# Last two heads of a grouped-query attention written as one sequence with three PSUM banks, in a two-layer hybrid attention kernel

## Chip, core and metric

The kernel runs on one core of a Trainium2 chip, as one launch. The metric is device time in microseconds: 1148.67 us is the median of 3 runs of the kernel before (1148.1 to 1149.11). TensorE (PE) multiplies matrices; its weight loads stand in a row of their own (PEld) and overlap the products. VectorE (DVE), ScalarE (ACT) and GpSimd (POOL) do the elementwise work, SyncE (SP) issues nearly all transfers. Each engine works through its own list of instructions in order. Products are summed in PSUM, which has eight banks of 128 x 512 fp32; the other tiles lie in SBUF.

## What is computed

Two layers act on 512 latent and 256 context tokens of width 1024. Each layer has a neighbourhood attention (branch a) and a grouped-query attention (branch b, 8 query heads on 2 key/value heads, 64 wide); both read all context keys. Each branch's output is multiplied by its own SiLU gate, projected, and the two are merged:

```python
def _merge(a_att, b_att, a_z, b_z, g_a, g_b, w_o_a, w_o_b, w_out):
    o_a = (a_att * jax.nn.silu(a_z)) @ w_o_a
    o_b = (b_att * jax.nn.silu(b_z)) @ w_o_b
    merged = jax.nn.sigmoid(g_a) * o_a + jax.nn.sigmoid(g_b) * o_b
    return merged @ w_out
```

The first layer also updates the context (its context queries read context keys alone), the second, which is the last, doesn't. So layer 0 works on 768 tokens, layer 1 on 512 wherever only queries are concerned.

## The kernel before

**Precision.** Each fp32 operand is split into a high part (a cast on ACT) and a low part (the rest, a subtraction on DVE or POOL), and a matrix product is three PE products: high x high, low x high, high x low (`mm3`, L351 to L353).

**The grouped-query attention** (called gq below, from L934 on) runs head by head in `pipeline` (L837). For head h, `gq_scores` makes four tiles of scores of 128 queries x 768 keys (L718, L719), DVE takes the row maximum (L955), ACT the exponential (L957), and DVE (L656) or POOL (L658, L659) scales the rows: POOL those of tiles 1 and 3 (`GQ_POOL`). One step later `gq_values` (L963) treats head h-1 in six **blocks** k of 128 keys: four PE transposes of the scaled tiles into one bank (L669), ACT's cast of that bank to `pth` (L672), DVE's subtraction to `ptl` (L673), and two products into the head's sum (L972, L973). In layer 0 a seventh block does the context queries (L746, L747). The transposes have two banks (`pst`), `pth` and `ptl` two buffers each. `head_out` (L675) ends a head: ACT copies half of the sum (L681), DVE adds the other half (L682), POOL multiplies into `zb` (L683), the gate of branch b.

**Filling products.** `fill` is a list of the remaining gate projections and of branch a's output projection (`o_chunks("a", ...)`, sums in `psf`, inputs `gah` and `gal`, evacuated on DVE in L592). `pipeline` runs an eighth of it per head, and all that is left ahead of head 7's values. A compiling scheduler then sets the order on each engine from the dependences and the order of the code, so filling products stand well ahead of where the code has them; `in_program_order` and `behind` can pin an order.

**After head 7**, `early` has loaded the gates of the merge (`tg`) and split the first three quarters of `zb` into `gbh` and `gbl` (`hilo`: ACT casts in L557, POOL subtracts in L558); the fourth quarter, heads 6 and 7, follows in L1002. Branch b's output projection (`o_chunks("b", ...)`: `gbh` and `gbl` by `w_o_b`, eight groups of 128 channels, four k steps of three products each) is evacuated by `evac_b` (L1005): DVE in L1007 and L1008, ACT in L1010, DVE in L1011. Its sums lie in a pool of five banks (`psx`) opened once the attention's banks are given back (`open_ps`), and in the one bank `psf`. Weights come by SP's queue; ACT casts (L336, L321) and DVE or POOL subtracts (L338, L324); `whi` and `wlo` have eight buffers each. Last comes the output projection of 128 tokens at a time (`tok_proj`, two halves of 512 columns), with `evac_o` (L1037): a DVE multiply (L1039), a DVE addition (L1041) and, in layer 1, the store (L1043).

## Time and profile before

| | |
|---|---|
| median of 3 runs | 1148.67 us (1148.1 to 1149.11) |
| the profiled execution | 1149.07 us |
| its span in the trace | 1147.0 us, so 2.07 us lie around it |
| granted TensorE clock | 0.999 |
| busy time | PE 1123.5, PEld 949.2, DVE 818.3, ACT 580.3, POOL 483.0 us |

A row of the timeline gives the start in us from the span's start, the duration, the engine and line, what is written from what, shapes and count; in brackets stands the idle time ahead of it and what ended it. PE's durations overlap: how long one product really takes is the distance to the next start. A row of the windows gives busy time and number of instructions of each engine in one stretch. A row of the waits gives the sum, the number of times and the longest.

### The profile page before, as it was taken

The page shows a single profiled execution, that of the slowest core. Times are in us where ns is not written, and L with a number is a line of the kernel's source. Part 1 is how long each engine was busy: PE and PEld are TensorE (multiplying, and loading weights), DVE is VectorE, ACT ScalarE, POOL GpSimd, SP SyncE. Part 2 cuts the span into 40 slices and gives each one's busy share as a digit, 9 for nine tenths or more (in the row PEclk, how much of TensorE's full clock was granted, in tenths as well). Part 3 has the DMA queues.
Part 4 walks back from the last instruction along what each step waited for, and adds up shares of the span by engine and source line. Part 5 has one row for each costly group of instructions (what it writes and reads, how often), then busy time and mean ns, then how long its engine had stood idle before and what let it go on. Part 6 is the DMA issues. An engine that isn't in the chain of part 4 may idle for free.

```text
span 1147.0 us, 17434 instructions
## 1 busy us (share of the span) xinstructions
PE 1123.5 (98%) x6136; PEld 949.2 (83%) x6136; DVE 818.3 (71%) x1533; ACT 580.3 (51%) x1185; POOL 483.0 (42%) x449
## 2 busy tenths in 40 slices
PE   7999999999999999999999999999999999999998
PEld 5788888888988888888788787888888888887786
DVE  6777688997454786697588755469787665898563
ACT  6553366655433565665330355336666355766421
POOL 1073355453374343453411227345554664465311
PEclk9999999999999999999999999999999999999999
DMA  9645311333322232451434424633332333152143
GB/s 370 232 127 156 90 51 60 105 110 111 106 101 89 95 103 92 92 221 38 149 127 130 151 70 122 193 89 115 97 113 74 111 102 101 65 176 90 61 133 92
DMA packets 89695, 135.08 MB, mean 118 GB/s; under 512 B 10789, under 2 KB 52745, under 8 KB 88969
## 3 DMA queue, kind: packets, MB, share of 16 engines
q1 hardware_dynamic: 89328, 133.87, 36.8%
q8 instruction: 48, 0.79, 0.3%
q14 instruction: 39, 0.31, 0.1%
q10 hardware_dynamic: 280, 0.12, 0.0%
HBM read 116.63 MB, written 17.32 MB: 117 GB/s over the span
## 4 chain that ended last, share of the span: by engine, by line
PE 80%; DVE 7%; DMA 4%; issue 3%; ACT 3%; POOL 2%; SPq 0%; POOLq 0%; ACTq 0%; DVEq 0%
PE psx L353 12%; PE psx L352 12%; PE psx L351 11%; PE psf L351 9%; PE psf L352 9%; PE psf L353 9%; PE pst L669 4%; DMA raw<-in_w_in_dram 2%; PE pss L718 2%; PE pss L719 2%; PE psv L973 2%; PE psv L972 1%; PE pss L795 1%; PE pst L431 1%; DMA rawb<-in_w_ada_dram 1%
## 5 line engine op out<-in xcount | busy, mean ns | idle before, releaser
L673 DVE TENSOR_TENSOR ptl<-pst,pth 128x512 fp32r<-128x512 f32 (+1 forms) x176 | 115.9, 671 | 46.4 <-ACT pth L672 45.4
L672 ACT CAST pth<-pst 128x512 fp32r<-128x512 f32 (+1 forms) x176 | 99.3, 577 | 86.7 <-PE pst L669 55.8
L338 POOL TENSOR_TENSOR wlo<-raw,whi 128x512 fp32r<-128x512 f32 x68 | 95.6, 1409 | 105.1 <-ACT whi L336 83.9
L351 PE MATMUL psf<-hx,whi 128*128 128x512 f32 (+1 forms) x368 | 139.2, 378 | 0.6 <-ACT zt L516 0.6
L352 PE MATMUL psf<-hx,whi 128*128 128x512 f32 (+1 forms) x368 | 138.2, 375 | 0.0
L353 PE MATMUL psf<-hx,wlo 128*128 128x512 f32 (+1 forms) x368 | 137.8, 374 | 0.0
L351 PE MATMUL psx<-whi,hx 128*128 128x512 f32 (+1 forms) x368 | 137.6, 375 | 0.0
L353 PE MATMUL psx<-whi,hx 128*128 128x512 f32 (+1 forms) x368 | 135.9, 369 | 0.1
L352 PE MATMUL psx<-wlo,hx 128*128 128x512 f32 (+1 forms) x368 | 135.7, 369 | 0.0
L336 ACT CAST whi<-raw 128x512 fp32r<-128x512 f32 x136 | 82.7, 621 | 51.6 <-DMA raw<-in_w_in_dram 35.6
L321 ACT CAST whi<-raw 128x512 fp32r<-128x512 f32 x88 | 53.9, 623 | 99.6 <-PE psx L353 38.1
L669 PE MATMUL pst<-ident,p 128*128 128x128 f32 x640 | 99.9, 272 | 1.4 <-DVE ptl L673 0.8
L324 POOL TENSOR_TENSOR wlo<-raw,whi 128x512 fp32r<-128x512 f32 x36 | 50.9, 1416 | 110.0 <-ACT whi L321 74.6
L338 DVE TENSOR_TENSOR wlo<-raw,whi 128x512 fp32r<-128x512 f32 x68 | 68.6, 1010 | 28.1 <-ACT whi L336 27.2
L669 PEld LDWEIGHTS pst<-ident,p 128*128 128x128 f32 x640 | 77.8, 140 | 13.0 <-DVE ptl L673 1.3
L658 POOL TENSOR_SCALAR r<-r 128x1 f32<-128x1 f32 x64 | 22.4, 350 | 152.2 <-DVE r L653 145.2
L659 POOL TENSOR_TENSOR p<-p,r 128x512 f32<-128x512 f32 (+1 forms) x64 | 84.2, 1316 | 5.1
L353 PEld LDWEIGHTS psx<-whi,hx 128*128 128x128 f32 x368 | 69.4, 189 | 12.6 <-DVE hx L1137 1.0
L351 PEld LDWEIGHTS psx<-whi,hx 128*128 128x128 f32 x368 | 69.5, 189 | 12.4 <-issue 0.8
L353 PEld LDWEIGHTS psf<-hx,wlo 128*128 128x128 f32 x368 | 69.4, 188 | 11.8
L351 PEld LDWEIGHTS psf<-hx,whi 128*128 128x128 f32 x368 | 69.4, 189 | 11.4 <-ACT zt L516 0.8
L352 PEld LDWEIGHTS psx<-wlo,hx 128*128 128x128 f32 x368 | 69.5, 189 | 10.8
(252 smaller groups left out, 3056.0 us busy)
## 6 DMA issues: line engine op xcount, KB each, us to landing
raw<-in_w_in_dram SPq DMA_DIRECT2D x168, 256.0 KB, 2.9
rawb<-in_w_ada_dram SPq DMA_DIRECT2D x64, 256.0 KB, 2.9
gs<-zt SPq DMA_DIRECT2D x32, 256.0 KB, 2.1
raw<-in_w_out_dram SPq DMA_DIRECT2D x32, 256.0 KB, 2.9
tg<-gs SPq DMA_DIRECT2D x4, 1536.0 KB, 6.8
rawx<-in_w_ada_dram SPq DMA_DIRECT2D x8, 512.0 KB, 7.9
raw<-in_w_o_a_dram SPq DMA_DIRECT2D x16, 256.0 KB, 2.8
raw<-in_w_o_b_dram SPq DMA_DIRECT2D x16, 256.0 KB, 2.8
```

The lines of the kernel that those rows point to most:

```text
L321: S.copy(hi[:, :n], raw[:, :n])
L324: e.tensor_tensor(lo[:, :n], raw[:, :n], F(hi[:, :n]), ALU.subtract)
L336: S.copy(hi, raw)
L338: lo_eng(i).tensor_tensor(lo, raw, F(hi), ALU.subtract)
L351: T.matmul(ps, lhs[0], rhs[0], start=first, stop=False)
L352: T.matmul(ps, lhs[0], rhs[1], start=False, stop=False)
L353: T.matmul(ps, lhs[1], rhs[0], start=False, stop=last)
L659: G.tensor_tensor(p[:, c0:c1], p[:, c0:c1], r[:, i:i + 1].to_broadcast([128, c1 - c0]), ALU.mult)
L669: T.transpose(pt[:, c0:c0 + 128], src, ident)
L672: S.copy(hi[:, n0:n1], pt[:, n0:n1])
L673: V.tensor_tensor(lo[:, n0:n1], pt[:, n0:n1], F(hi[:, n0:n1]), ALU.subtract)
L718: T.matmul(ps[:, c0:c0 + n], q, sl(kh), start=True, stop=False)
```

## The change

**Heads 6 and 7.** `pipeline` gets a `tail`. After head 7's scores it calls `gq_tail`, which has both heads' values as one list of blocks: six of head 6, in layer 0 the two heads' context blocks, six of head 7. Three banks and three pairs of buffers go round: the two `pst` banks and one of the score banks; the third pair comes from the weights' `whi` and `wlo`. Three blocks are transposed and split in advance, and block b+3 is transposed behind the products of block b. What is left of `fill`, and behind it the steps of `early`, stand among the first five blocks. The products of the first three o_b groups, k steps 0 to 2, follow the last block; then the fourth quarter of `gbh` and `gbl` and their last k step. PE, ACT and DVE keep the written order in this stretch. For these two heads DVE does the multiplies into `zb` (was POOL) and the last subtraction of `gbl`; the weights of the first two o_b chunks are loaded ahead of the tail with POOL's subtraction; POOL scales head 7's tiles 0 and 2 instead of 1 and 3.

**Last token tile** of layer 1's last half: two sums of 256 columns with an evacuation and a store each.

```diff
+                    if h == 7 and tail is not None:
+                        run(bg, len(bg))
+                        return tail(prev, st, fill, last)
...
-                    softmax_tail(p, 768, r[:, 0:1], [(0, 768)], G if i in GQ_POOL else None)
+                    softmax_tail(p, 768, r[:, 0:1], [(0, 768)], G if i in ((0, 2) if att["h"] == 7 else GQ_POOL) else None)
...
+            lead = [(f, 0, 512) for f in range(3)]
...
+            def gq_tail(st6, st7, fill, after):
+                need_wb(0, pool_lo)
...
+                banks = [psw(512, "t"), psw(512, "t"), psw(512, "s")]
+                s1 = psw(512, "s")
+                extra = fill + after
...
+                parts = [[att["p"].tile([128, 512], F32R, tag=t, name=nm(t), bufs=att["nt"]) for t in ("pth", "ptl")]
+                         for i in range(2)]
+                parts.append([wp.tile([128, 512], F32R, tag=t, name=nm(t), bufs=8) for t in ("whi", "wlo")])
+                po6 = psw(512, "v")
...
+                def gate_part(c0, c1):
+                    hi, lo = [a[:, 3, c0:c1] for a in gated["b"]]
+                    S.copy(R(hi), zv[:, 3, c0:c1])
+                    V.tensor_tensor(R(lo), zv[:, 3, c0:c1], hi, ALU.subtract)
...
+                def turn_block(b):
+                    if b < len(blocks):
+                        pt, (hi, lo) = banks[b % 3], parts[b % 3]
+                        for src, c0 in blocks[b][0]:
+                            T.transpose(pt[:, c0:c0 + 128], src, ident)
+                        S.copy(hi, pt)
+                        V.tensor_tensor(lo, pt, F(hi), ALU.subtract)
+                for b in range(3):
+                    turn_block(b)
+                for b, (_, mm, out) in enumerate(blocks):
+                    mm(*parts[b % 3])
+                    turn_block(b + 3)
+                    if out:
+                        out()
+                    run(extra, -(-len(extra) // max(5 - b, 1)) if b < 5 else 0)
+                    if first and b == 9:
+                        gate_part(512, 768)
+                for (f, n0, n1), ps in zip(lead, (po6, s1, psw(512, "s"))):
+                    chan_mm(ps, wb[f // 2], f % 2, act_b, n0, n1, 0, 3)
+                    open_sums.append((f, n0, n1, ps))
+                gate_part(0, 512)
+                in_program_order((ON_PE, ON_ACT, ON_DVE), nc.cur_bb.bb.instructions[at:], {ON_PE: before.name})
+                for f, n0, n1, ps in open_sums:
+                    chan_mm(ps, wb[f // 2], f % 2, act_b, n0, n1, 3, 4)
...
+            for f, n0, n1, ps in open_sums:
+                evac_b(f, n0, n1, ps)
...
+                    if not first and n == 1 and t == nt - 1:
+                        for c in ((0, 256), (256, 512)):
+                            ps = psw(256)
+                            tok_mm(ps, [[a[:, c[0]:c[1]] for a in x] for x in w], 256, a_m, t, 0, KT)
+                            evac_o(t, ps, c=c)
+                        break
```

What moves, at three places. In the rows the line number stands first, then the operation, out<-in with the tiles' numbers, and the shape; line numbers of the change are its own (L671 was L669, L979 and L980 were L972 and L973, L1072 to L1074 are the new blocks).

**PE, layer 1, values of head 5.** `psv` is the head's sum, `pth` and `ptl` a block's two parts, `pst` a transposed block, `psf<-gbh` a filling product. Before:

```order
L351 MATMUL psf_11903<-gbh_11785,whi_11879 128x512
L972 MATMUL psv_11504<-pth_11532,vb_9741 128x512
L973 MATMUL psv_11504<-ptl_11533,vb_9741 128x512
L972 MATMUL psv_11504<-pth_11543,vb_9741 128x512
L669 MATMUL pst_11549<-ident,p_11295 128x128
L669 MATMUL pst_11549<-ident,p_11307 128x128
L669 MATMUL pst_11549<-ident,p_11320 128x128
L669 MATMUL pst_11549<-ident,p_11332 128x128
L973 MATMUL psv_11504<-ptl_11544,vb_9741 128x512
```

With the change, at the same blocks:

```order
L979 MATMUL psv_11470<-pth_11509,vb_9707 128x512
L671 MATMUL pst_11515<-ident,p_11261 128x128
L671 MATMUL pst_11515<-ident,p_11273 128x128
L671 MATMUL pst_11515<-ident,p_11286 128x128
L671 MATMUL pst_11515<-ident,p_11298 128x128
L980 MATMUL psv_11470<-ptl_11510,vb_9707 128x512
L671 MATMUL pst_11526<-ident,p_11261 128x128
L671 MATMUL pst_11526<-ident,p_11273 128x128
L671 MATMUL pst_11526<-ident,p_11286 128x128
L671 MATMUL pst_11526<-ident,p_11298 128x128
L979 MATMUL psv_11470<-pth_11520,vb_9707 128x512
L980 MATMUL psv_11470<-ptl_11521,vb_9707 128x512
```

The 36 `psf<-gah` and 6 `psf<-gbh` products that stood from head 4's fourth block to head 5's last are gone from there; the 36 stand behind blocks 0 and 1 of the tail, and none behind the later ones.

**ACT, layer 0, last blocks.** `pth` and the tail's `whi<-pss` are casts of transposed blocks, `gbh` a cast of the gated values, `whi<-raw` a cast of weights, `ho` and `zt` the copies of `head_out`. Before:

```order
L681 COPY ho_6263<-psv_6258 64x256
L672 CAST pth_6377<-pst_6372 128x512
L672 CAST pth_6388<-pst_6383 128x512
L336 CAST whi_6628<-raw_6626 128x512
L336 CAST whi_6634<-raw_6632 128x512
L672 CAST pth_6399<-pst_6394 128x512
L672 CAST pth_6410<-pst_6405 128x512
L672 CAST pth_6425<-pst_6420 128x512
```

With the change:

```order
L1073 CAST whi_6210<-pss_6204 128x512
L559 CAST gbh_6329<-zb_4186 128x768
L336 CAST whi_6537<-raw_6535 128x512
L336 CAST whi_6594<-raw_6592 128x512
L1073 CAST pth_6206<-pst_6202 128x512
L559 CAST gbh_6329<-zb_4186 128x768
L1073 CAST pth_6208<-pst_6203 128x512
L559 CAST gbh_6329<-zb_4186 128x768
L1073 CAST whi_6210<-pss_6204 128x512
L684 COPY ho_6361<-psv_6212 64x512
L1073 CAST pth_6206<-pst_6202 128x512
L684 COPY zt_6375<-pss_6205 64x256
```

The three casts of gated values stand between the casts of blocks 5 to 8, and two casts of weights ahead of block 6's.

**DVE, layer 1, evacuation of the o_b groups.** `tg<-tg,psf` is the evacuation of a sum, `tg<-tg,tg` the addition of the branches, `wlo` weights. Before:

```order
L682 TENSOR_TENSOR ho_11860<-psv_11793,ho_11860 64x512
L1007 SCALAR_TENSOR_TENSOR tg_11781<-tg_11781,psf_11903 128x512
L1007 SCALAR_TENSOR_TENSOR tg_11781<-tg_11781,psx_11920 128x512
L324 TENSOR_TENSOR wlo_12081<-raw_12077,whi_12079 128x512
L1008 TENSOR_TENSOR tg_11269<-tg_11269,tg_11781 128x512
L1007 SCALAR_TENSOR_TENSOR tg_11781<-tg_11781,psx_11949 128x512
```

With the change:

```order
L686 TENSOR_TENSOR zb_10275<-zb_10275,ho_11824 64x512
L1060 TENSOR_TENSOR gbl_11758<-zb_10275,gbh_11757 128x512
L324 TENSOR_TENSOR wlo_12019<-raw_12015,whi_12017 128x512
L1098 SCALAR_TENSOR_TENSOR tg_11753<-tg_11753,psv_11668 128x512
L1098 SCALAR_TENSOR_TENSOR tg_11753<-tg_11753,pss_11661 128x512
L1099 TENSOR_TENSOR tg_11235<-tg_11235,tg_11753 128x512
L1098 SCALAR_TENSOR_TENSOR tg_11753<-tg_11753,pss_11828 128x512
```

The first three sums lie in attention banks (`psv`, two `pss`) instead of `psx` banks, and the third is evacuated fourth of the four rows that read or add them; the first `psx` sum behind them takes the bank of `pss_11828`.

## Prediction

> **What bounds the kernel now.** I read the page's head first, then PE's waits by cause, the windows of the three stretches that the change touches, and the timelines inside them. The page's busy times and, below them, rows of the waits (sum, times, longest) say how much there is to win:

> ```profile
> span 1147.0 us, 17434 instructions
> PE 1123.5 (98%) x6136; PEld 949.2 (83%) x6136; DVE 818.3 (71%) x1533; ACT 580.3 (51%) x1185; POOL 483.0 (42%) x449
> ...
> PE psx L1150 <- DMA ident<-in_ident_dram: 4.7, 1, 4.7
> PE psv L973 <- DVE ptl L673: 2.0, 3, 1.5
> ...
> PE psx L351 <- DVE ho L682: 1.2, 1, 1.2
> ...
> PE psf L352 <- POOL gbl L558: 0.8, 1, 0.8
> ```

> PE is busy 98% of the span, 23.5 us are idle, and 4.7 of these lie at the start, where nothing changes. The second row is a wait inside this attention, the third and fourth stand behind it in layer 0. The windows (length, then busy time and count of PE, PEld, DVE, ACT and POOL, granted clock, DMA share, GB/s) are layer 0's last two heads, layer 1's values of heads 4 and 5 from where the changed order first differs, and layer 1's last two heads:

> ```profile
> 528.50:559.75 31.25, 30.47 (x190) 26.22 (x189) 21.79 (x37) 17.71 (x34) 14.16 (x11) 1.00 0.08 26
> 1040.70:1062.98 22.28, 20.74 (x113) 17.02 (x111) 18.63 (x29) 13.26 (x27) 11.96 (x12) 1.00 0.22 69
> 1062.98:1078.12 15.14, 13.91 (x72) 9.49 (x71) 9.57 (x14) 8.39 (x15) 4.31 (x4) 1.00 0.06 15
> ```

> The clock is full in all three, so only pace and waits count. In the second window DVE is the fullest engine beside PE, 18.63 of 22.28 us. PE's real prices are distances between starts:

> ```profile
> 1062.01 0.60 PE L669 MATMUL pst<-ident,p 128*128 128x128 f32 x4
> 1062.36 0.48 PE L972 MATMUL psv<-pth,vb 128*128 128x512 f32 x1
> ...
> 1064.01 0.66 PE L669 MATMUL pst<-ident,p 128*128 128x128 f32 x4 [0.43 <-DVE ptl L673]
> 1064.73 0.49 PE L972 MATMUL psv<-pth,vb 128*128 128x512 f32 x1
> 1065.07 0.40 PE L973 MATMUL psv<-ptl,vb 128*128 128x512 f32 x1
> 1065.30 0.39 PE L972 MATMUL psv<-pth,vb 128*128 128x512 f32 x1
> ...
> 1078.12 0.40 PE L351 MATMUL psx<-gbh,whi 128*128 128x512 f32 x1
> 1078.36 0.39 PE L352 MATMUL psx<-gbl,whi 128*128 128x512 f32 x1
> ```

> Four transposes take 0.35 (1062.01 to 1062.36), the product behind them 0.34 (1064.73 to 1065.07), a product behind a product 0.23. A block on PE is thus about 0.35 + 0.33 + 0.23 = 0.9 us. The same block on the other engines:

> ```profile
> 1062.64 0.59 ACT L672 CAST pth<-pst 128x512 fp32r<-128x512 f32 x1 [0.79 <-PE pst L669]
> 1063.26 0.69 DVE L673 TENSOR_TENSOR ptl<-pst,pth 128x512 fp32r<-128x512 f32 x1 [0.68 <-ACT pth L672]
> ```

> From the transposes' start at 1062.01 the cast starts 0.63 later, the subtraction 0.62 after that, and at 1064.01 PE has its bank back: 2.0 us for the round. Two banks give a block every 1.0 us, a little slower than PE's 0.9; three give one every 0.67.

> **Layer 1, ahead of the tail.** Of the 22.28 us, 42 products leave (36 into the tail, 6 behind it). At 0.23 they take 9.6 us with them, so an unchanged kernel would spend 12.7 us on the rest. What DVE does there:

> ```profile
> 1049.19 0.67 DVE L592 SCALAR_TENSOR_TENSOR tg<-tg,psf 128x512 f32<-128x512 f32 x1
> ...
> 1050.39 1.81 DVE L955 TENSOR_REDUCE mx<-pss 128x1 f32<-128x768 f32 x2
> ...
> 1054.28 0.62 DVE L656 TENSOR_SCALAR p<-p,r 128x768 f32<-128x768 f32 x1
> ...
> 1057.96 1.28 DVE L673 TENSOR_TENSOR ptl<-pst,pth 128x512 fp32r<-128x512 f32 x2
> ```

> The evacuation of a sum (0.67) goes with the products that leave. By the other rows there remain ten subtractions at about 0.64, five maxima at 0.9, two scalings at 0.62, `head_out`'s addition and five short reciprocals, together some 13 us. The covering products gone, DVE is as long as PE's whole stretch, and the two cannot be laid side by side, since a block goes PE, ACT, DVE, PE within two banks. A maximum of 0.9 us in front of a subtraction then holds the next block; PE waited up to 1.5 us for that `ptl` even with the 42 products in between (the second waits row). I let four of the five maxima (3.6) and half of the addition (0.4) show: +4.0. The ends are 1.2 (only the start and the last maximum show) and 5 (all of it shows).

> **Layer 1, the tail.** Before's 15.14 us hold 3 products that move out (0.7), so 14.4 are to be compared. PE's own time for twelve blocks is 12 x 0.9 = 10.8; the 36 products that come in cost their 8.3 us, which the stretch ahead has given back already. Steady state is free of waits: three blocks on PE take 2.7, the round takes 2.0. At the end it isn't: the last two blocks have no transposes behind them, so block 10's round is covered by 1.8 us and block 11's by 1.4, which leaves 0.2 + 0.6. With 0.5 for head 7's first blocks, whose scaled tiles come late, the tail takes 12.1: -2.3. The ends are -3.6 (PE's pace) and -1.4 (DVE, which also has two multiplies into `zb` and the last `gbl` now, shows by another 0.9).

> **Layer 1, behind the tail.** The 27 products of the lead (6.2 us) and seven of the `psf` sum cover head 7's `head_out`, cast and last subtraction, so these cost nothing; without that cover they would cost what layer 0 shows today, 1.2. But the three sums lie in attention banks now, and the first `psx` sum must wait until the third has been read. From the first sum's last product PE has nine products (2.1 us) till then. DVE needs four rows (sum, sum, addition, sum) like that at 1049.19, 0.67 alone and some 0.64 apart in a row (the pair at 1057.96 takes 1.28): 2.6, with 0.4 of hand-over at the two ends 3.0 us: +0.9. It costs 0.3 if the scheduler's rows start early and 1.8 if DVE is still busy with its weights row.

> **Layer 0.** Here I read PE, ACT, DVE and POOL around the end of the stretch:

> ```profile
> 535.83 0.84 ACT L557 CAST gbh<-zb 128x768 fp32r<-128x768 f32 x1 [0.65 <-POOL zb L683]
> ...
> 561.30 0.36 ACT L681 COPY ho<-psv 64x256 f32<-64x256 f32 x1 [3.08 <-POOL zb L683]
> 561.70 0.43 DVE L682 TENSOR_TENSOR ho<-psv,ho 64x256 f32<-64x256 f32 x1 [2.63 <-ACT ho L681]
> ...
> 562.18 0.50 PE L351 MATMUL psx<-gbh,whi 128*128 128x512 f32 x1 [1.20 <-DVE ho L682]
> ```

> Nine products move behind the window (2.1 us), so 31.25 becomes 29.2 to compare, and the 0.8 us wait for `gbl` goes: 28.4. Seven pieces of filling stay, but they stand among blocks 0 to 3 of fourteen; ten blocks are bare. There ACT has eight or more block casts at 0.59, three casts of gated values at 0.84, two of weights and the copies of `head_out`: some 9 us against PE's ten blocks at 0.9, so each gated cast delays a block cast and with it PE. I let half of the three show (1.3), and the last two blocks as in layer 1 (0.8): 30.5, or +1.3. The ends are -1.1 and +2.5. The 1.20 us wait at 562.18 is `head_out`, now under the lead: -1.2. The bank wait is there too, and the products that cover it are partly half as wide:

> ```profile
> 530.03 0.28 PE L351 MATMUL psf<-gah,whi 128*128 128x256 f32 x1
> 530.15 0.28 PE L352 MATMUL psf<-gal,whi 128*128 128x256 f32 x1
> ```

> Four of 512 and six of 256 columns (0.12 each) cover 1.6 of the 3.0 us: +1.3 (0.5 to 2.2). Layer 0 together: +1.4.

> **The last token tile.** The end of the program:

> ```profile
> 1141.17 0.39 PE L353 MATMUL psx<-whi,ml 128*128 128x512 f32 x1
> 1141.60 0.69 DVE L1039 TENSOR_TENSOR t<-psx,gate 128x512 f32<-128x512 f32 x1 [3.80 <-PE psx L353]
> 1142.32 0.69 DVE L1041 TENSOR_TENSOR xt<-xt,t 128x512 f32<-128x512 f32 x1
> 1143.04 0.54 SPq L1043 DMA_DIRECT2D out_dram<-xt  x1
> ```

> With 256 columns the two DVE rows take 0.42 each (the 256-wide addition above has 0.43): -0.54. PE pays 48 x 0.12 for 24 x 0.23: +0.24. The first half's evacuation and store lie under the second's products, and from the issue to the end of the span (3.96 us) I expect no change: -0.3 (-0.8 to +0.2).

> **What costs nothing.** The weights of two chunks go ahead of the tail with POOL's subtraction; they are needed only at the lead, and POOL is busy 11.96 of 22.28 us there. That POOL scales other tiles of head 7 shifts one scaling between engines of equal need.

> **Sum.** +4.0 - 2.3 + 0.9 + 1.4 - 0.3 = +3.7 us on the profiled execution's 1149.07, which is 0.4 above the median: 1148.67 + 3.7 = 1152.4. A difference of 0.2% (2.3 us) is about what a measurement can tell from none.

> **Rivals.**

> *Everything hides* (faster). If DVE's queue between 1040.7 and 1063 falls below PE's own pace, near 11 us, three banks bring what they promise: -1.7 there, the tail at 10.8 (-3.6), no bank wait, layer 0 at -0.8 - 1.2, the end -0.3: -7.6, so 1141.1. For it speaks that the 12.7 holds PE's waits of today; against it DVE's 18.63 us and its 13 by count. [...]

> *It cancels* (same). DVE packs its rows (+1.2), the tail gains its 2.3, the bank wait is 0.3, layer 0 shows only its last blocks (28.4 + 0.8 - 29.2 = 0, -1.2, bank +0.6), the end -0.3: -1.7, so 1147.0. The ends of my largest term are far apart, which speaks for it.

> *DVE is held by POOL* (slower still). The moved multiplies and the last `gbl` have two inputs in SBUF, on the engine that everything in the tail passes:

> ```profile
> 1045.06 0.68 DVE L338 TENSOR_TENSOR wlo<-raw,whi 128x512 fp32r<-128x512 f32 x1
> ...
> 1056.02 1.47 POOL L659 TENSOR_TENSOR p<-p,r 128x768 f32<-128x768 f32 x1
> 1056.29 1.75 DVE L338 TENSOR_TENSOR wlo<-raw,whi 128x512 fp32r<-128x512 f32 x1
> ```

> Beside POOL's row the same subtraction takes 1.07 longer than alone. Three such meetings in the two tails add 3.2: 1155.6. It decides if POOL works while DVE's two-input rows stand in the tail; against it, POOL has only 4.31 of 15.14 us there. [...]

> **How the numbers follow.** I give my forecast 0.46 (its own range 1151 to 1155), the cancelling 0.29, everything hidden 0.18, the held DVE 0.07. Faster holds the hidden case and an edge of the cancelling one, slower the forecast and the held DVE. The range takes in the forecast, the cancelling case and the lower half of the held one, and leaves out most of the hidden case: 1145.0 to 1156.0.

> **What would show it.** Right: the stretch from 1040.7 to the first tail block takes near 17 us, with PE waiting for `ptl`; the tail with its 36 products near 20.4; a wait of about 1 us of the first `psx` sum for the third sum's evacuation; layer 0's wait for `ho` gone. Wrong: the stretch of head 5 near 12 us would give the cancelling or the hidden case; DVE rows over 1 us in the tail the last one. The forecast as a whole falls if the time is under 1149.

## The result, and the profile after

The changed kernel takes 1162.3 us (median of 4 runs, 1160.93 to 1162.52) against 1148.38 (4 runs): 1.0118 times as long, 95% interval 1.0100 to 1.0135. It is slower, as forecast, but by 13.9 us instead of 3.7, and outside the range of 1145.0 to 1156.0. One execution of one experiment (1248.82 us at a granted clock of 0.851, the run with the filling ahead in both layers) is left out of what is said of it.

The page's head and the waits of PE, to be laid beside those of before:

```profile
span 1160.0 us, 17492 instructions
...
PE 1128.0 (97%) x6160; PEld 954.0 (82%) x6160; DVE 824.7 (71%) x1540; ACT 579.9 (50%) x1186; POOL 479.2 (41%) x445
```

```profile
PE pss L1048 <- DVE zt L685: 4.5, 1, 4.5
PE psf L351 <- DVE tg L594: 3.6, 4, 1.5
PE psv L980 <- DVE ptl L675: 2.4, 6, 0.8
PE psx L351 <- DVE tg L1098: 2.4, 2, 1.4
...
PE psf L1036 <- DVE ptl L1074: 1.0, 2, 0.8
```

The first row is new, a single wait of 4.5 us. `ho L682` and `gbl L558`, 1.2 and 0.8 us in the kernel before, are gone. Laying the same PE instructions of the two profiles on each other, the distance between them is -0.2 us at 528, +10.8 at 648, +9.2 at head 5 of layer 1, and 13.0 at the end of the span. So layer 0's last two heads, to which I gave 1.4 us, made most of it. Their stretch, which I forecast at 30.5 us, takes 39.94 (columns as in the prediction's windows: length, busy time and count of PE, PEld, DVE, ACT and POOL, granted clock, DMA share, GB/s):

```profile
528.34:568.28 39.94, 32.61 (x182) 27.19 (x180) 25.35 (x41) 17.45 (x35) 12.28 (x9) 0.91 0.07 20
```

Where the 4.5 us are, on PE, then DVE, then POOL:

```profile
554.75 0.60 PE L1072 MATMUL pst<-ident,p 128*128 128x128 f32 x4
559.84 0.58 PE L1048 MATMUL pss<-pth,vb 128*128 128x256 f32 x1 [4.49 <-DVE zt L685]
...
560.86 1.05 PE L1072 MATMUL pst<-ident,p 128*128 128x128 f32 x4
561.57 0.78 PE L1035 MATMUL psf<-whi,vb 128*128 128x512 f32 x1
562.14 0.63 PE L1036 MATMUL psf<-wlo,vb 128*128 128x512 f32 x1
```

```profile
555.91 0.68 DVE L685 TENSOR_TENSOR ho<-psv,ho 64x512 f32<-64x512 f32 x1
556.62 2.23 DVE L686 TENSOR_TENSOR zb<-zb,ho 64x512 f32<-64x512 f32 x1
558.78 0.67 DVE L1074 TENSOR_TENSOR ptl<-pst,pth 128x512 fp32r<-128x512 f32 x1
559.38 0.40 DVE L685 TENSOR_TENSOR zt<-pss,zt 64x256 f32<-64x256 f32 x1
```

```profile
554.75 3.56 POOL L560 TENSOR_TENSOR gbl<-zb,gbh 128x768 fp32r<-128x768 f32 x2
```

Head 7's context block writes the other half of the tile that holds head 6's context sum, so it waits until DVE has read that sum (`zt`, 559.38). Ahead of that read DVE has head 6's multiply into `zb`, which takes 2.23 us and ends just after POOL's two subtractions. And after the wait PE is slow: transposes that take 0.35 us at 553.34 take 0.71 here (560.86 to 561.57). The windows show why:

```profile
554.86:559.84 4.98, 0.49 (x5) 0.25 (x3) 4.54 (x6) 1.87 (x4) 3.45 (x2) 0.91 0.31 99
559.84:565.89 6.05, 6.05 (x23) 5.24 (x24) 2.63 (x5) 2.00 (x4) 0.00 (x0) 0.51 0.00 0
```

The granted clock is 0.51 for 6.05 us. The same work, four products of 256 columns and three blocks, takes 4 x 0.12 + 3 x 0.9 = 3.2 us at full clock: behind the wait another 2.9 us are lost.

Layer 1's head 5 stretch, from the place that stood at 1040.70 to the second transposed block of heads 6 and 7, where the forecast cut it too, and the tail up to the first lead product:

```profile
1049.97:1065.97 16.00, 13.04 (x70) 9.27 (x69) 13.11 (x24) 10.15 (x21) 6.29 (x7) 1.00 0.00 0
1065.97:1088.20 22.23, 19.90 (x106) 15.54 (x104) 12.20 (x19) 10.71 (x20) 7.63 (x6) 1.00 0.11 36
```

My sums were 12.7 + 4.0 = 16.7 and 12.1 + 8.3 = 20.4. The first is 0.7 too long, the second 1.8 too short. Behind the tail, PE, DVE and POOL:

```profile
1098.90 0.39 PE L353 MATMUL psf<-gbh,wlo 128*128 128x512 f32 x1
1100.70 0.50 PE L351 MATMUL psx<-gbh,whi 128*128 128x512 f32 x1 [1.41 <-DVE tg L1098]
```

```profile
1097.29 0.69 DVE L1098 SCALAR_TENSOR_TENSOR tg<-tg,psv 128x512 f32<-128x512 f32 x1 [0.24 <-PE psv L353]
1097.89 0.68 DVE L1098 SCALAR_TENSOR_TENSOR tg<-tg,pss 128x512 f32<-128x512 f32 x1
1098.49 1.56 DVE L1099 TENSOR_TENSOR tg<-tg,tg 128x512 f32<-128x512 f32 x1
1099.97 0.67 DVE L1098 SCALAR_TENSOR_TENSOR tg<-tg,pss 128x512 f32<-128x512 f32 x1
```

```profile
1098.21 1.28 POOL L324 TENSOR_TENSOR wlo<-raw,whi 128x512 fp32r<-128x512 f32 x1 [4.61 <-ACT whi L321]
```

The wait for the third sum's bank is there, 1.41 against my 0.9: the addition in between takes 1.56 us beside POOL's subtraction; the next addition, at 1100.57, takes 0.68.

### The profile page after: what moved, and what is told of

Read it like the earlier page. It is cut to its first block, busy times and chain, and to the rows that moved or that the text cites. A ratio compares the mean times of both kernels' runs of the same rounds, so it can differ in the third digit from the quotient of the medians.

```text
span 1160.0 us, 17492 instructions
## 1 busy us (share of the span) xinstructions
PE 1128.0 (97%) x6160; PEld 954.0 (82%) x6160; DVE 824.7 (71%) x1540; ACT 579.9 (50%) x1186; POOL 479.2 (41%) x445
## 4 chain that ended last, share of the span: by engine, by line
PE 82%; DVE 8%; issue 3%; DMA 2%; ACT 2%; POOL 1%; SPq 0%; POOLq 0%; DVEq 0%; ACTq 0%
PE psx L351 12%; PE psx L353 12%; PE psx L352 12%; PE psf L351 9%; PE psf L352 9%; PE psf L353 9%; PE pst L671 4%; PE pss L721 2%; PE pss L722 2%; PE pss L798 1%; PE pst L433 1%; DMA rawb<-in_w_ada_dram 1%; PE psv L980 1%; PE psv L979 1%; DVE ptl L675 1%
## 5 line engine op out<-in xcount | busy, mean ns | idle before, releaser
L338 POOL TENSOR_TENSOR wlo<-raw,whi 128x512 fp32r<-128x512 f32 x72 | 100.7, 1402 | 113.9 <-ACT whi L336 88.8
L351 PE MATMUL psx<-whi,hx 128*128 128x512 f32 (+1 forms) x376 | 140.9, 377 | 0.0
L351 PE MATMUL psf<-hx,whi 128*128 128x512 f32 (+1 forms) x368 | 139.2, 378 | 0.0
L353 PE MATMUL psx<-whi,hx 128*128 128x512 f32 (+1 forms) x376 | 138.8, 369 | 0.0
L352 PE MATMUL psx<-wlo,hx 128*128 128x512 f32 (+1 forms) x376 | 138.5, 369 | 0.0
L352 PE MATMUL psf<-hx,whi 128*128 128x512 f32 (+1 forms) x368 | 138.1, 375 | 0.0
L353 PE MATMUL psf<-hx,wlo 128*128 128x512 f32 (+1 forms) x368 | 137.8, 374 | 0.0
L675 DVE TENSOR_TENSOR ptl<-pst,pth 128x512 fp32r<-128x512 f32 (+1 forms) x150 | 98.4, 669 | 37.2 <-ACT pth L674 36.3
L674 ACT CAST pth<-pst 128x512 fp32r<-128x512 f32 (+1 forms) x150 | 84.2, 575 | 71.6 <-PE pst L671 46.8
L324 POOL TENSOR_TENSOR wlo<-raw,whi 128x512 fp32r<-128x512 f32 x36 | 52.6, 1463 | 138.3 <-ACT whi L321 125.1
L671 PE MATMUL pst<-ident,p 128*128 128x128 f32 x536 | 84.2, 272 | 1.2 <-DVE ptl L675 0.6
L338 DVE TENSOR_TENSOR wlo<-raw,whi 128x512 fp32r<-128x512 f32 x64 | 63.3, 991 | 29.8 <-ACT whi L336 29.5
L351 PEld LDWEIGHTS psx<-whi,hx 128*128 128x128 f32 x376 | 71.0, 189 | 12.5 <-issue 0.8
L353 PEld LDWEIGHTS psx<-whi,hx 128*128 128x128 f32 x376 | 70.9, 189 | 12.2
L352 PEld LDWEIGHTS psx<-wlo,hx 128*128 128x128 f32 x376 | 71.0, 189 | 11.0
L353 PEld LDWEIGHTS psf<-hx,wlo 128*128 128x128 f32 x368 | 69.4, 188 | 11.8
L351 PEld LDWEIGHTS psf<-hx,whi 128*128 128x128 f32 x368 | 69.4, 188 | 10.8 <-ACT zt L518 0.3
L352 PEld LDWEIGHTS psf<-hx,whi 128*128 128x128 f32 x368 | 69.4, 189 | 10.5
```

Source lines behind the costliest of these rows:

```text
L324: e.tensor_tensor(lo[:, :n], raw[:, :n], F(hi[:, :n]), ALU.subtract)
L338: lo_eng(i).tensor_tensor(lo, raw, F(hi), ALU.subtract)
L351: T.matmul(ps, lhs[0], rhs[0], start=first, stop=False)
L352: T.matmul(ps, lhs[0], rhs[1], start=False, stop=False)
L353: T.matmul(ps, lhs[1], rhs[0], start=False, stop=last)
L671: T.transpose(pt[:, c0:c0 + 128], src, ident)
```

## Experiments

Theory A, formed from these rows: one bank's wait and the slow clock behind it make layer 0's loss. Its rival B: the bare blocks do, and the wait only collects what they would lose.

**Head 6's context block first.** Six blocks now lie between the two users of the bank.

```diff
-                main_blocks(6, st6[0])
                 if first:
                     ctx_block(6, st6[1], s1[:, 0:256])
+                main_blocks(6, st6[0])
+                if first:
                     ctx_block(7, st7[1], s1[:, 256:512])
```

> Layer 0's list of blocks begins with head 6's context block instead of having it seventh, so that six blocks lie between the two context blocks, whose sums are halves of one bank. Theory A (one wait and its aftermath make layer 0's loss): the 4.49 us wait of head 7's context block for DVE's reading of head 6's context sum goes, and with it the 6.05 us behind it in which the granted clock is 0.51, which cost about 3.0 us; so 4.5 + 3.0 = 7.5 us less than 1162.3, about 1155, and the granted clock stays near 1.00 through the tail. Theory B (the unfilled blocks are bound by ACT and DVE, and the wait only collects what would be waited for anyway): at most 2 us less, 1160 or more, with other waits for ptl in its place.

1160.16 us, ratio 1.0096 (1.0081 to 1.0111). The bank's wait is gone, but only 2.1 of the 7.5 us came. A as I had put it fails. The time is now lost in another wait. DVE's queue in this kernel, and PE behind it:

```profile
537.82 0.69 DVE L1075 TENSOR_TENSOR wlo<-pss,whi 128x512 fp32r<-128x512 f32 x1 [1.57 <-ACT whi L1074]
538.43 0.68 DVE L1075 TENSOR_TENSOR ptl<-pst,pth 128x512 fp32r<-128x512 f32 x1
539.03 0.41 DVE L685 TENSOR_TENSOR zt<-pss,zt 64x256 f32<-64x256 f32 x1
539.47 1.40 DVE L686 TENSOR_TENSOR zb<-zb,zt 64x256 f32<-64x256 f32 x1
540.79 0.40 DVE L594 SCALAR_TENSOR_TENSOR tg<-tg,psf 128x256 f32<-128x256 f32 x1
```

```profile
541.25 0.50 PE L351 MATMUL psf<-gah,whi 128*128 128x512 f32 x1 [3.25 <-DVE tg L594]
```

The context sum's addition and its multiply (1.40 us beside a POOL row; a multiply of that size takes 0.42 alone, in the change at 559.82) stand ahead of the evacuation of a filling sum, and PE's next filling product waits 3.25 us for it. The granted clock is 0.50 from 542.69 to 546.10.

**Multiplies into `zb` by POOL.** The block order stays as in the change.

```diff
-                                                         zv[64 * e:64 * e + 64, 3, 0:512], None, V))
+                                                         zv[64 * e:64 * e + 64, 3, 0:512], None, G))
...
-                        head_out(po, e, zv[64 * e:64 * e + 64, 3, 512:768], t1, V)
+                        head_out(po, e, zv[64 * e:64 * e + 64, 3, 512:768], t1, G)
```

> POOL does the multiplies into zb of heads 6 and 7 again, as in the kernel before; the blocks' order stays. Theory A with the two engines' rows holding each other: head 6's multiply on DVE (2.23 us beside POOL's subtraction of gbl, 0.69 alone) no longer stands ahead of the reading of the context sum, so the 4.49 us wait becomes about 2.3. If the low clock behind it comes with a long wait only, it goes too: 1162.3 - 2.2 - 3.0 = 1157; if it comes with any wait of that place, 1160. Theory B: within 1 us of 1162.3.

1160.04 us, 1.0099 (1.0084 to 1.0114): the wait became 2.2 us, as expected, and the slow clock came all the same (0.50 from 558.29 to 561.70). So 2.3 us of the wait are the multiply. The median hides that the gain in layer 0 is larger: by the profiles layer 0 is 2.9 us shorter than in the change and the rest 1.3 longer, since the first `psx` sum of layer 1 now waits 2.08 us and the clock is at 0.50 from 1097.59 to 1101.01 there too.

**Second context block moved back.** Head 6's context block and its place in DVE's queue stay; head 7's now stands behind four blocks of head 7 (the text below says three).

```diff
                 if first:
                     ctx_block(6, st6[1], s1[:, 0:256])
-                    ctx_block(7, st7[1], s1[:, 256:512])
                 main_blocks(7, st7[0])
+                if first:
+                    ctx_block(7, st7[1], s1[:, 256:512])
+                    blocks.insert(11, blocks.pop())
...
-                    if first and b == 9:
+                    if first and b == 12:
```

> Head 6's context block stays seventh in layer 0's list, so DVE's queue at that place is the same as in the change, but head 7's context block moves behind three blocks of head 7: the second user of the bank comes four blocks later. Theory A: the 4.49 us wait and the slow clock behind it go, 1162.3 - 7.5 = 1154.8. Theory C (what PE waits for there is DVE's queue, whoever is waiting: head 6's multiply of 2.23 us beside POOL stands ahead of the next blocks' subtractions too): some 2 us of the wait come back as a wait for ptl, 1157, and 1160 if the low clock comes with it.

1158.38 us, 1.0085 (1.0072 to 1.0099). With the multiply left where the change has it, the block's place is worth 3.9 us. Theory C, that DVE's queue is what is waited for, is nearer: PE waits 2.16 us for a `ptl`.

```profile
556.91 0.48 PE L1035 MATMUL psf<-pth,vb 128*128 128x512 f32 x1
559.55 0.53 PE L1036 MATMUL psf<-ptl,vb 128*128 128x512 f32 x1 [2.16 <-DVE ptl L1076]
```

The slow clock isn't there in every execution of this kernel: two show a granted clock of 0.998 (1158.63, the profiled one, and 1159.92 us), two of 1.000 (1158.05 and 1158.13). On the average that is 1.2 us.

**And head 6's multiplies on POOL.** `None, V` becomes `None, G if h == 6 else V`, and `t1, V` likewise.

> As the run with the second context block moved back, and POOL does head 6's two multiplies into zb again (head 7's stay on DVE). By theory A nothing more is to be had: the same time within 0.7 us. By theory C DVE's queue loses the 2.23 us row, and this one is 2 us or more below the other.

1153.57 us, 1.0040 (1.0027 to 1.0054): 4.8 us below the one before, 8.7 below the change, and 3.9 below the one before in the profiles' layer 0. C holds. No slow clock is left (granted 1.00 in the stretch).

**Instead, the multiply on DVE and POOL's rows later.** This tells whether it is the row's place in the queue or POOL's company.

```diff
-                extra = fill + after
+                extra = fill + (after[:1] if first else after)
+                split = after[1:] if first else []
...
+                    if first and b in (7, 8):
+                        split[b - 7]()
```

> As the run with the second context block moved back, head 6's multiply into zb still on DVE, but the last two splits of gated values (ACT's casts and POOL's subtractions of 1.75 us each, 554.75 to 558.3) start two or three blocks later in layer 0. Theory D (DVE's two-input row is held while POOL's runs): the multiply takes its 0.7 us instead of 2.28, the 2.16 us wait for ptl goes to 0.6 or less and no slow clock follows: about 1154, as with the multiply on POOL. Rival E (the place in DVE's queue is what costs, not POOL): the multiply's row and the wait stay, 1157 or more.

1154.08 us, 1.0043 (1.0030 to 1.0057): as good, with head 6's multiply still on DVE and in the same place of its queue.

```profile
554.51 0.68 DVE L685 TENSOR_TENSOR ho<-psv,ho 64x512 f32<-64x512 f32 x1
555.23 0.68 DVE L686 TENSOR_TENSOR zb<-zb,ho 64x512 f32<-64x512 f32 x1
555.84 0.67 DVE L1077 TENSOR_TENSOR ptl<-pst,pth 128x512 fp32r<-128x512 f32 x1
```

```profile
553.46 1.84 POOL L560 TENSOR_TENSOR gbl<-zb,gbh 128x768 fp32r<-128x768 f32 x1 [0.43 <-ACT gbh L559]
556.90 3.89 POOL L560 TENSOR_TENSOR gbl<-zb,gbh 128x768 fp32r<-128x768 f32 x2 [1.60 <-ACT gbh L559]
```

From 555.30 to 556.90 POOL is idle, and there the multiply takes 0.68 instead of 2.23 us. Theory D holds and E falls, with one reservation: ACT's two casts moved too. In the change, DVE's row just ahead of the multiply, 0.68 us at 555.91, runs beside the same subtractions and isn't lengthened; one of its two inputs lies in PSUM, while the multiply has both in SBUF. Three rows with both inputs in SBUF took longer beside POOL than alone: 2.23 against 0.68, 1.40 against 0.42 and 1.56 against 0.68. By what POOL holds them isn't shown.

**One filling piece ahead of the third block.** The second context block is moved back here too.

```diff
-                for b in range(3):
+                for b in range(2):
                     turn_block(b)
+                run(extra, 1)
+                turn_block(2)
```

> As the run with the second context block moved back, and one filling piece runs between the second and the third of the blocks turned in advance. The third pair of buffers comes from the weights' slots, and the slot is read by the first filling piece in the list; ACT's cast of the third block waited for that piece (3.50 us idle, till 537.40 in the profile of the change), and behind it DVE's subtractions and the evacuation that the next piece waits for (1.50 us at 537.91 in layer 0, 0.98 at 1071.14 in layer 1). If the borrowed slot makes these waits, this is 1.5 to 2.5 us below the other; if DVE's queue makes them anyway, within 0.5 us.

1156.14 us, 1.0064 (1.0050 to 1.0077), 2.2 below the run with the second context block moved back, as expected. The profiles show the gain in layer 1: from the tail's first transposed block to the first lead product it takes 21.78 instead of 23.92 us, and two waits of the other run are gone:

```profile
1063.68 0.50 PE L1035 MATMUL psv<-pth,vb 128*128 128x512 f32 x1 [0.58 <-DVE ho L685]
...
1068.61 0.50 PE L351 MATMUL psf<-gah,whi 128*128 128x512 f32 x1 [1.00 <-DVE tg L594]
```

In layer 0 the waits for filling sums are 1.22 + 0.78 + 0.78 instead of 1.50 + 0.51, no less. The piece frees the borrowed slot earlier, but it also covers the wait for `ho` and puts the evacuation of its own sum earlier into DVE's queue; which of these the gain comes from isn't shown.

**The tail in layer 1 alone.** Layer 0 has the code of before.

```diff
-            pipeline(fill, 8, gq_first, values_of(zb, gq_values), early, bg, gq_tail)
+            pipeline(fill, 8, gq_first, values_of(zb, gq_values), early, bg, gq_tail if has_tail else None)
```

> Layer 0 as in the kernel before, layer 1 as in the change, the last tile in two parts. By the profiles the two kernels' layer 0 differ by 10.8 us and the rest by 2 to 4, so 1162.3 - 10.8 = 1151.5 if the layers add up (my forecast for layer 1 alone was 1148.67 + 4.0 - 2.3 + 0.9 - 0.3 = 1151.0). The rival, that layer 1's loss depends on what layer 0 leaves in the queues, would give under 1149 or over 1154.

1151.94 us, 1.0030 (1.0019 to 1.0042): the layers add up. Layer 0 costs 10.4 us, layer 1 with the split tile 3.2.

**Filling ahead of the tail, in both layers.**

```diff
                         run(bg, len(bg))
+                        run(fill, len(fill))
                         return tail(prev, st, fill, last)
```

> All that is left of the filling products stands ahead of the tail in the code (so in layer 1 the 36 products go back among the blocks of heads 4 and 5), the tail keeps three banks and no filling products. If the removed cover costs what I forecast, head 5's stretch in layer 1 gains about 3.3 us (its waits go back from 6.4 to 3.0 us), the tail's waits for the evacuation of filling sums (1.0 us in layer 1, 1.5 + 0.5 in layer 0) go, and the tail's bare blocks cost some 1 to 2 us more: 1162.3 - 3.3 - 3.0 + 2 = 1158. If filling products among the tail's blocks are worth as much there as ahead, no change: 1162.

1157.37, 1158.14 and 1161.28 us, 1.0096 (1.0076 to 1.0116). The middle one is 4.2 us below the change, as expected, but they lie far apart, and the granted clock goes with them: 1.000, 0.999 and 0.997. The profile is that of the fastest. In its layer 1 the distance to the kernel before stays at 9.1 us from head 5 to the products behind the tail, so the tail costs nothing there; in layer 0 it is still 10.7. There the wait for the bank is 2.98 us and no slow clock follows, but the filling products, with no blocks in between, wait five times for the evacuation of their sums, 4.1 us together.

**Filling ahead, tail in layer 1 alone.** The last two edits together.

> The tail in layer 1 alone, with all filling products ahead of it, in their old places; the last tile in two parts. If layer 1's loss is the cover taken from heads 4 and 5, the 3.2 us of the tail in layer 1 alone turn to -1 (in the run with the filling ahead in both layers layer 1 from its head 5 to its end cost nothing, and the split tile gives 0.7): 1151.9 - 4.3 = 1147.6. If what the tail's blocks lose without filling is as much as what heads 4 and 5 gain: 1150 or more.

1147.19 us, 0.9986 (0.9977 to 0.9995): 4.75 us below the tail in layer 1 with its filling inside. Layer 1's two stretches, cut as above:

```profile
1038.61:1059.49 20.88, 20.15 (x106) 15.94 (x105) 16.05 (x27) 10.36 (x21) 6.29 (x7) 1.00 0.00 0
1059.49:1072.11 12.62, 11.70 (x70) 8.85 (x68) 10.09 (x16) 10.30 (x20) 8.05 (x6) 1.00 0.23 64
```

Without the 36 filling products at 0.23, head 5's stretch is 12.6 us, where the change has 16.00: the cover is worth 3.4. The tail is 12.6 us, where the change has 22.23 - 8.3 = 13.9: the filling products among its blocks cost 1.3 us more than their own time. Together this is 4.7 of the 4.75, so layer 1's loss is explained.

**And the three lead sums read in a row**, DVE's order pinned.

```diff
+            at = len(nc.cur_bb.bb.instructions)
             for f, n0, n1, ps in open_sums:
-                evac_b(f, n0, n1, ps)
+                b = tg_part(1, f, n0, n1)
+                V.scalar_tensor_tensor(b, b, 1.0, ps, ALU.add, ALU.mult)
+            for f, n0, n1, ps in open_sums:
+                evac_b(f, n0, n1, None)
+            if open_sums:
+                in_program_order((ON_DVE,), nc.cur_bb.bb.instructions[at:], {})
```

> As the one before, and DVE reads the three lead sums in a row before it adds any of them, so that the bank of the third comes free one row (0.6 us) earlier. PE's wait of the first psx sum (1.41 us) becomes 0.8 if that row is what ends it: 1147.0. If PE waits for the sums' last products or for DVE's start, no change.

1145.79 us, 0.9972 (0.9962 to 0.9983), the fastest kernel here and 3.0 us faster than before. The wait didn't shrink by a row, it went: the row that stood in between was the addition, 1.56 us beside POOL. PE's waits in this kernel, in which no `tg` of the merge is left:

```profile
PE pst L669 <- DVE ptl L675: 1.5, 3, 0.8
PE psf L351 <- ACT zt L518: 1.3, 2, 1.1
PE psx L351 <- DVE ho L685: 1.2, 1, 1.2
PE psf L352 <- POOL gbl L560: 0.8, 1, 0.8
PE psv L982 <- DVE ptl L675: 0.8, 2, 0.6
```

**All of it in both layers** (second context block back, head 6's multiplies on POOL, filling ahead in layer 1, sums in a row).

> All that the runs favoured, in both layers: the second context block moved back, head 6's multiplies on POOL, layer 1's filling ahead of the tail, the three lead sums read in a row. From 1153.57: -4.3 for the filling, -0.6 in each layer for the sums: 1148.1. If that holds, three banks are worth no more than the old order; the three-bank tail in layer 1 alone would be the better one by about 1 us.

1146.84 us, 0.9984 (0.9975 to 0.9993). This is 1.3 us less than the text's sum; the difference of about 1 us to the tail in layer 1 alone came. So layer 0's tail, mended, still costs about 1 us against the old order there.

**The split tile alone**, on the kernel before.

> The kernel before with nothing but the last token tile in two parts. My term was -0.3 us (1148.4). In the change's profile the span ends 4.56 us after the last product's start, in the one before 5.83 us: by that -1.3 + 0.25 for PE = -1.0 (1147.7).

1148.11 us, 0.9992 (0.9983 to 1.0001): -0.7, between my -0.3 and the profile's -1.0; the interval includes no change at all.

## Why the prediction was wrong

**The side was right, the size not.** The steps of layer 1 carried in the main. "Ahead of the tail" was +4.0 and is +3.4 (16.00 us against 22.28 less 9.7 for 42 products), and the filling put back gave 3.4 there. "The tail" was -2.3 and is -0.5 (13.9 against 14.4). The three banks do bring most of what was forecast, -1.8, when no filling stands among the blocks (12.6); with it PE waits, 0.98 us of it for the evacuation of a filling sum, a row that I hadn't priced inside the tail. "Behind the tail" was +0.9 and is +1.4; the mechanism was right, and the addition took 0.88 us longer beside POOL. The last tile was -0.3 and is about -0.7. Together these are +3.6 where 3.2 were measured.

**Layer 0 is the step that failed.** I wrote "30.5, or +1.3" from ACT's casts and "+1.4" for the layer; it cost 10.4. The other two terms of that sum came about as said: the wait for `ho` is gone (-1.2), and the bank behind the tail costs 1.0 against +1.3. The stretch itself took 39.94 us instead of 30.5, +10.7 instead of +1.3. Its limit was not ACT but DVE's queue, and three things are missing in the step. The second context block shares its tile with the first, so PE waits for a read that stands behind everything in DVE's queue; moving that block back brought 3.9 us. The multiply that the change moves to DVE meets POOL's subtractions exactly there: 4.3 to 4.8 us more, shown from both sides, by moving the multiply and by moving POOL's rows. And the wait cost more than its length, as the clock fell to 0.50 behind it: 2.9 us more in the change. How the loss divides between the block and the multiply depends on which is mended first (the multiply first brought 2.3, in layer 0 2.9); both together it doesn't: the two runs without either stand 8.2 and 8.7 us below the change.

**The rival had the cause and I priced it away.** "DVE is held by POOL" got 0.07 and 3.2 us. I argued against it with POOL's 4.31 us of 15.14, a figure of layer 1's window; the meeting is in layer 0, where POOL's subtractions of `gbl`, 1.8 us each, follow the casts that the change itself puts among the blocks. I had read those casts on ACT and didn't follow them to POOL. And I priced the meetings as DVE's loss of 1.07 each, without asking what PE does meanwhile.

**What stays open.** Of layer 0's 10.4 us, 8.2 to 8.7 are settled; the rest is about as long as the waits for filling sums in the tail (1.50 and 0.51), and no run removed these alone. Whether the third pair's borrowed weight slot costs anything was not settled either: the cast into it waited 3.50 us in the change, and the run that moved a filling piece ahead of it is 2.1 us shorter in layer 1's tail but moved other rows too. A pair of its own wasn't tried.

## What to carry over

Follow each moved instruction to every engine that it sets in motion: a cast on ACT brings its subtraction on POOL, and a multiply on DVE with both inputs in SBUF took 2.23 us beside POOL against 0.68 without. In an order that is pinned, a late row delays all that stands behind it (the read that PE waited 4.49 us for stood behind that multiply), so look for what PE reads or overwrites next in that queue. Filling products were worth most where another engine was the slow one: taken from there, they were missed by 3.4 us, and among blocks that three banks already covered they cost 1.3.

## What was not expected of the hardware

```profile
555.51:558.93 3.42, 0.00 (x0) 0.00 (x0) 3.38 (x4) 1.25 (x3) 2.80 (x2) 1.00 0.31 94
558.93:562.34 3.41, 2.50 (x10) 2.40 (x11) 1.27 (x3) 0.39 (x1) 0.00 (x0) 0.50 0.00 0
562.34:565.75 3.41, 3.41 (x14) 2.81 (x13) 2.23 (x4) 1.48 (x4) 0.00 (x0) 0.50 0.00 0
```

```profile
539.28:542.69 3.41, 1.44 (x6) 1.23 (x7) 1.88 (x3) 0.00 (x0) 1.27 (x1) 1.00 0.23 74
542.69:546.10 3.41, 3.41 (x9) 2.54 (x9) 0.52 (x1) 0.00 (x0) 0.00 (x0) 0.50 0.03 8
```

```profile
557.41:560.83 3.42, 1.95 (x13) 1.44 (x13) 3.07 (x5) 2.89 (x6) 3.42 (x3) 1.00 0.21 70
560.83:564.24 3.41, 1.73 (x13) 1.60 (x14) 2.04 (x4) 0.52 (x1) 0.14 (x1) 1.00 0.00 0
```

What the falls go with is PE's idle time inside one such stretch. Ahead of the falls it was 3.42 us in the change, 1.97 with the context block first, 2.20 and 2.08 with POOL's multiplies, 2.16 with the second block moved back. The wait of 2.98 us in the run with the filling ahead was cut in two, the stretches are idle for 1.47 and 1.68 us, and the clock stayed full. All stretches of the kernel before and of the change, cut in this way, show the same: behind those idle for up to 1.53 us (before, from 1056.54) no fall came, and behind one idle throughout, after the last product, it came in both (1145.29 and 1159.67). So the stretch needn't have been idle throughout: 1.97 us of 3.41 were enough in the run with the context block first. And the same kernel cost more in one execution than in the next: with the second block moved back, the two executions at a clock of 0.998 took 1.2 us more on the average than the two at 1.000. What sets the length of these stretches and where they lie isn't shown.
